# Filler matmuls in the waits of a router and sort, and a later turn back of the logits

## The chip, the cores and the metric

The kernel runs on one core of a Trainium2 chip. The metric is the time of one execution on the device, in microseconds (us). The core has five engines with a queue each: TensorE (PE, with its weight loads as PEld), VectorE (DVE), ScalarE (ACT), GpSimd (POOL) and the sync engine (SP), which here issues nearly all loads from HBM. An engine works through its queue in order, and waits where an instruction needs what another engine has not done yet.

## What is computed

Two layers of a decoder for 512 tokens of width 1024. The part of the reference that matters here is the mixture of experts that ends each layer: a router picks one of 4 groups and in it 2 of 8 experts for each token, the assignments are sorted by expert, and each expert works on its tokens.

```
for l in range(DEPTH):
    ...
    x = layer_norm(ALPHA * x + mixed @ w_out[l], ln_gain[l, 0], ln_bias[l, 0])
    ffn = hierarchical_moe(x, router_group_w[l], ...)
    x = layer_norm(ALPHA * x + ffn, ln_gain[l, 1], ln_bias[l, 1])

def hierarchical_moe(x, wg, bg, we, be, w_gate, w_up, w_down):
    g_logit = (xt @ wg) + bg
    _, g_idx = lax.top_k(g_logit, 1)
    e_logit = take_along_axis((xt @ we + be).reshape(n, 4, 8), g_idx)
    top_logit, top_local = lax.top_k(e_logit, 2)
    expert = g_idx * EXPERTS_PER_GROUP + top_local
    order = jnp.argsort(expert.reshape(n_assign), stable=True)
    counts = jnp.bincount(e_flat, length=N_EXPERTS)
    ...
    hdn = silu(xb @ w_gate[e]) * (xb @ w_up[e])
    return hdn @ w_down[e]
```

## The kernel before

**Tiles and stages.** The tokens lie in four tiles t = 0 to 3 of 128 rows. A layer has a dense part (projection, mixers, output projection, normalisation, router) and an expert part. The expert part first takes two fixed experts, whose weights are loaded ahead, and then 12 rounds of two or three experts each. Which experts those are is in `ids`, a small table that the sort of each layer makes; the sync engine reads it and only then issues the loads of a round's weights, each a tile of 1 MB, into 18 slots that come free as TensorE finishes with what lies in them.

**The loop over the tiles.** The second half of the output projection of a tile is a list of eight steps of three matmuls each (`gemm(t)`, `run(steps, n)` runs the next n). While TensorE runs the steps of tile t + 1, VectorE and ScalarE add and normalise tile t (`begin`, `over`; the last scaling is L934 and L935), TensorE turns the rows of tile t (`turned`, L1074, copied by L1082 and L1084), and `logits` multiplies them with the router's weights (L1093), one tile later. The logits come out with the experts along the partitions; VectorE copies them (L1098), and `back` turns them again (L1105, L1106), from where VectorE copies them into `L` (L1107). `choose` is a chain of ten small VectorE steps per tile that finds group and experts (L1134 to L1129).

**Router's end and sort.** After the last tile, `early` takes one PSUM bank `rp` from the four banks called g; columns 0 to 127 take the ranks of the four tiles (`rank`, L1170 and L1171), and further columns the counts and the sort's results (`count_up` L1177 and L1179, `sort_a` L1210 and L1211, `sort_b` L1223). VectorE reads that bank in `ranks` (L1185), `keys` (L1203, L1204), `sort_b` (L1218, L1221, L1222) and `sort_c`, whose first copy is `ids` (L1228). `onehots` (L1290) makes the one-hot rows that the first matmuls of the expert part need, the gather (L1330). The fixed experts' matmuls are L1370 and, after them, L1401.

**Order.** All of this is under a manual schedule: each engine's queue stands in the order in which the program is written, and the framework adds the waits that the use of tiles asks for. `warm(n)` puts n matmuls of the identity with itself into a fresh bank g whose result nobody reads; each is two MATMUL rows of the trace.

Of the kernel before, what the change touches and what calls it, by code (L numbers as in the profile page):

```python
# [162 lines left out]
class Trunk:  # L163
# [700 lines left out]
    def output(self, l):  # L864
# [47 lines left out]
        def gemm(t):  # L912

            ps = self.s()
            c = slice(128 * t, 128 * t + 128)

            def step(q, k):
                nc.tensor.matmul(ps, mh[:, k, c], wh[:, k, :], start=(q == 0), stop=False)
                nc.tensor.matmul(ps, mh[:, k, c], wl[:, k, :], start=False, stop=False)
                nc.tensor.matmul(ps, ml[:, k, c], wh[:, k, :], start=False, stop=(q == 7))  # L920

            return ps, [lambda q=q, k=k: step(q, k) for q, k in enumerate(korder)]

        def run(steps, n=99):
            while steps and n > 0:
                n -= 1
                steps.pop(0)()

        def over(t):
            st = sums[t]  # L930
            nm, sd, rs, nb = (st[:, n : n + 1] for n in (2, 4, 5, 6))
            V.reciprocal(rs, sd)
            V.tensor_mul(nb, nm, rs)
            V.tensor_scalar(self.xh(t, 0), self.xh(t, 0), nm, rs, OP.add, OP.mult)  # L934
            A.activation(self.xh(t, 1), self.xh(t, 1), AF.Identity, bias=nb, scale=rs)  # L935
# [27 lines left out]
        def begin(t, ps):  # L963
            add(t, 1, ps)
            apart(t, 1)

            st = sums[t]
            V.tensor_scalar(st[:, 7:8], st[:, 0:1], st[:, 1:2], 1.0 / (UP * D), OP.subtract, OP.mult)
            V.scalar_tensor_tensor(st[:, 5:6], st[:, 7:8], st[:, 7:8], st[:, 5:6], OP.mult, OP.add)
            self.centre(t, st)  # L970
            A.activation(st[:, 4:5], st[:, 4:5], AF.Sqrt, bias=st[:, 5:6], scale=UP**-2 / D)

        def rows(t, *engines):

            for h in range(2):
                high(t, h)
            for h in range(2):
                low(t, h, engines[h])
            for row, op in zip(tabs, (OP.mult, OP.add)):
                for h in range(2):  # L980
                    self.by_row(P, t, h, row, op)

        with self.manual(ET.PE):
            ps, steps = gemm(0)
            run(steps)
            for t in range(NT):
                last = t == NT - 1
                begin(t, ps)
                if not last:
                    ps, steps = gemm(t + 1)  # L990
                if t > 0:
                    lt = self.logits(t - 1, xt)
                if last:
                    self.back(2, lt)
                run(steps, 2)
                over(t)
                if 0 < t < 3:
                    self.back(t - 1, lt)
                if t == 2:
                    self.choose((0, 1))  # L1000
                if last:
                    self.choose((2,))
                    self.warm(6)
                run(steps, 4)
                xt = self.turned(t, A, A if last else V)
                rows(t, *((P, P) if last else (V, V)))
                run(steps)
            A.activation(sums[3][:, 3:4], self.eps, AF.Exp)
            self.warm(2)
            lt = self.logits(3, xt)  # L1010
            self.early()
            self.back(3, lt)
            self.warm(8)
            self.choose((3,), [lambda: self.ranks(0, 3)])
            self.oh16 = f[:, 5, :].bitcast(F16).rearrange("p (a t s) -> p a t s", a=2, t=NT)
            self.count_up()
            self.rank(NT - 1)
            self.keys()
            self.sort_a()
            self.places()  # L1020
            self.sort_b()
            self.warm(8)
            self.onehots(slice(0, 2))
            self.sort_c()
            self.onehots(slice(2, 4))
# [80 lines left out]
        nc.tensor.matmul(ps[:, 0:36], lt, self.two, start=False, stop=True)  # L1106
        nc.vector.tensor_copy(self.L[:, t, :], ps[:, 0:36])  # L1107

    def warm(self, n):

        if n:
            ps = self.g()
        for _ in range(n):
            self.nc.tensor.matmul(ps[:, 0:128], self.ident, self.ident, start=True, stop=True)

    def choose(self, tiles, more=()):

# [718 lines left out]
```

## Time and profile before

| | before |
|---|---|
| median of 3 runs | 1513.57 us (1512.85 to 1513.63) |
| profiled execution | 1514.36 us |
| its span, first to last instruction | 1512.7 us |
| TensorE busy | 1362.2 us (90%) |
| VectorE busy | 689.1 us (46%) |
| ScalarE busy | 395.2 us (26%) |
| GpSimd busy | 153.1 us (10%) |
| mean granted clock of TensorE | 0.956 |
| read from HBM | 441.45 MB, 293 GB/s over the span |

The times of the rows further down are counted from the start of the span. A granted clock of 1.00 is 2.4 GHz and 0.50 is 1.2 GHz, the two levels that TensorE's clock has. The profile divides the span into 40 slices of 37.8 us.

### The profile page before, as it was taken

What the parts mean: (1) busy time and instruction counts of PE and PEld (TensorE: products, weight loads), DVE (VectorE), ACT (ScalarE), POOL (GpSimd) and SP (SyncE); (2) the same over time, 40 slices, a digit from 0 to 9 for tenths busy, and PEclk for the clock granted to TensorE, in tenths of its full rate; (3) what the DMA queues carried; (4) which work ended last, traced back from release to release, by engine and by line L of the source; (5) the groups of instructions that cost most, each with busy time, mean ns of one, the idle gap of its engine ahead of it and who ended that gap; (6) DMA issues with size and microseconds to landing.
All of it is one profiled execution on the core that took longest, in us unless ns stands there. A gap on an engine that the chain in (4) does not pass through costs nothing. (4 is left out here: it accounts for less than half of the span.)

```text
span 1512.7 us, 22662 instructions
## 1 busy us (share of the span) xinstructions
PE 1362.2 (90%) x8836; PEld 755.1 (50%) x8837; DVE 689.1 (46%) x1540; ACT 395.2 (26%) x720; POOL 153.1 (10%) x188
## 2 busy tenths in 40 slices
PE   8999997899998988999699998979999989889994
PEld 7876576534343434343378665866343424343431
DVE  4347758524423242422553676585344242424225
ACT  5446544111010101011364555341110101010112
POOL 1112205100000000000141221050000000000001
PEclk9999999899999999999899998988999999999997
DMA  9410250799999999999911025408999999999994
GB/s 346 143 56 1 102 205 28 306 381 420 420 419 422 420 421 412 420 422 412 382 65 59 1 82 189 149 29 321 389 420 420 419 421 421 421 413 421 420 408 166
DMA packets 84550, 445.15 MB, mean 294 GB/s; under 512 B 8080, under 2 KB 14352, under 8 KB 36816
## 3 DMA queue, kind: packets, MB, share of 16 engines
q1 hardware_dynamic: 83184, 440.15, 72.5%
q0 software_dynamic: 960, 2.90, 0.6%
q8 instruction: 74, 1.21, 0.3%
q10 hardware_dynamic: 288, 0.52, 0.1%
q14 instruction: 44, 0.36, 0.1%
HBM read 441.45 MB, written 2.10 MB: 293 GB/s over the span
## 5 line engine op out<-in xcount | busy, mean ns | idle before, releaser
L1370 PE MATMUL g<-w,f 128*32 128x512 f32 (+1 forms) x3072 | 399.6, 595 | 13.7 <-DMA w<-expert_w_up 9.4
L1370 PEld LDWEIGHTS g<-w,f 128*32 128x32 f32 (+1 forms) x3072 | 120.8, 112 | 248.1 <-issue 202.4
L1401 PE MATMUL g<-w,f 128*32 128x512 f32 (+1 forms) x1536 | 211.6, 653 | 29.2 <-ACT f L1390 10.1
L1424 DVE TENSOR_TENSOR X<-X,s 128x512 f32<-128x512 f32 x176 | 113.0, 683 | 256.7 <-PE s L1419 256.7
L1401 PEld LDWEIGHTS g<-w,f 128*32 128x32 f32 (+1 forms) x1536 | 58.3, 121 | 161.7 <-issue 131.2
L1412 DVE SCALAR_TENSOR_TENSOR y<-g,gv,y 128x512 fp32r<-128x512 f32 x52 | 38.9, 750 | 212.1 <-ACT y L1411 209.8
L1419 PE MATMUL s<-y,fa 128*128 128x512 f32 x416 | 126.7, 425 | 6.4 <-DVE X L1424 3.5
L1419 PEld LDWEIGHTS s<-y,fa 128*128 128x128 f32 x416 | 70.1, 189 | 103.8 <-issue 71.9
L1411 ACT ACTIVATE y<-g,gv 128x512 fp32r<-128x512 f32 x52 | 35.5, 687 | 215.7 <-PE g L1401 215.7
L1330 PE MATMUL t<-fa,mh 128*128 128x256 f32 (+1 forms) x448 | 79.0, 298 | 8.9 <-ACT f L1390 8.8
L1341 ACT ACTIVATE f<-t,pp 128x256 f32<-128x256 f32 (+1 forms) x56 | 30.7, 549 | 206.7 <-PE t L1330 206.7
L1339 DVE TENSOR_SCALAR f<-t,pp 128x256 f32<-128x256 f32 (+1 forms) x56 | 29.4, 525 | 93.1 <-ACT f L1341 93.1
L1330 PEld LDWEIGHTS t<-fa,mh 128*128 128x128 f32 x448 | 61.3, 191 | 15.4 <-ACT f L1390 11.7
L1330 PE MATMUL t<-f,x1l 128*128 128x256 f16 (+1 forms) x448 | 64.9, 267 | 0.0
L1382 ACT ACTIVATE f<-g 128x512 f32<-128x512 f32 x26 | 15.6, 599 | 183.1 <-PE g L1370 183.1
L1530 POOL DMA_DIRECT2D rows<-ln_gain x2 | 1.1, 548 | 614.2 <-DMA w<-expert_w_gate 307.2
L1390 ACT COPY f<-t 128x512 f32<-128x512 f32 x26 | 15.2, 585 | 167.7 <-PE t L1389 167.7
L404 POOL TENSOR_TENSOR X<-X,f 128x512 f32<-128x512 f32 x32 | 40.5, 1296 | 87.9 <-DVE x1l L948 82.4
L404 POOL TENSOR_TENSOR X<-X,E 128x512 f32<-128x512 f32 x11 | 16.3, 1486 | 306.2 <-ACT X L1696 154.6
L701 ACT ACTIVATE f<-f,nm 128x128 f32<-128x128 f32 (+3 forms) x64 | 35.7, 558 | 43.7 <-POOL nm L700 42.9
L371 DVE TENSOR_TENSOR fa<-w,fa 128x512 fp32r<-128x512 f32 (+1 forms) x36 | 31.3, 877 | 32.0 <-ACT fa L370 31.9
L700 POOL TENSOR_SCALAR nm<-mx 128x1 f32<-128x1 f32 x64 | 22.3, 352 | 180.6 <-DVE mx L697 119.0
(338 smaller groups left out, 2165.5 us busy)
## 6 DMA issues: line engine op xcount, KB each, us to landing
w<-expert_w_gate SPq DMA_DIRECT2D x128, 1024.0 KB, 19.8
w<-expert_w_up SPq DMA_DIRECT2D x128, 1024.0 KB, 19.8
w<-expert_w_down SPq DMA_DIRECT2D x116, 1024.0 KB, 19.8
w<-w_in SPq DMA_DIRECT2D x20, 1024.0 KB, 13.6
w<-expert_w_down SPq DMA_DIRECT2D x48, 256.0 KB, 5.3
w<-w_out SPq DMA_DIRECT2D x8, 1024.0 KB, 5.3
X<-x SPq DMA_DIRECT2D x4, 512.0 KB, 5.9
w<-w_in SPq DMA_DIRECT2D x4, 512.0 KB, 8.2
```

The costliest lines, as they stand in the source:

```text
L371: self.nc.vector.tensor_sub(lo, src, hi.bitcast(F32))
L404: e.tensor_tensor(out=x, in0=x, in1=row[:, 512 * h : 512 * h + 512], op=op)
L701: nc.scalar.activation(p, p, AF.Exp, bias=nm, scale=0.125, accum_out=den)
L1330: nc.tensor.matmul(ps[:, w * j : w * j + w], src[:, k, 128 * t : 128 * t + 128], one[:, 0:n, t, :], start=(i == 0), stop=(i == 2 * NT - 1),)
L1339: nc.vector.tensor_scalar(xg[:, k, 0:w], src, gain(k), bias(k), OP.mult, OP.add)
L1341: nc.scalar.activation(xg[:, k, 0:w], src, AF.Identity, bias=bias(k), scale=gain(k))
L1370: nc.tensor.matmul(pss[m][a:b, :], xs[:, k, a:b], w[m][e][:, k, :], start=(k == 0), stop=(k == 7),)
L1401: nc.tensor.matmul(pss[hf][a:b, :], hT[:, 128 * j + a : 128 * j + b], part(e, hf, j), start=(j == 0), stop=(j == 3),)
L1411: nc.scalar.mul(yh, ps, gv)
L1412: nc.vector.scalar_tensor_tensor(yl, ps, gv, yh.bitcast(F32), OP.mult, OP.subtract)
L1419: nc.tensor.matmul(ps, oT[:, 128 * t : 128 * t + 128], y[q], start=(q == 0), stop=(q == 1))
L1424: nc.vector.tensor_add(x, x, ps)
```

## The change

In the loop four steps of the next tile's output products, instead of two, stand between the logits and their turn back, and two instead of four between that and the turn of the rows. `warm` can be given a place to write. Ahead of the turn back of tile 2 stand eight new filler matmuls, in a fresh bank g. After the turn back of tile 3 stand 24 instead of 8, ahead of `sort_a` 3, ahead of `sort_b` 8, and behind `sort_b` 14 instead of 8; all of these write columns 384 to 511 of the bank `rp`. Lines below L991 move by one to four, so that L1185 becomes L1189, L1218 becomes L1222 and L1228 becomes L1232.

```diff
                 if t > 0:
                     lt = self.logits(t - 1, xt)
                 if last:
+                    self.warm(8)
                     self.back(2, lt)
-                run(steps, 2)
+                run(steps, 4)
                 over(t)
                 if 0 < t < 3:
                     self.back(t - 1, lt)
...
                 if last:
                     self.choose((2,))
                     self.warm(6)
-                run(steps, 4)
+                run(steps, 2)
                 xt = self.turned(t, A, A if last else V)
...
             self.back(3, lt)
-            self.warm(8)
+            spare = self.rp[:, 384:512]
+            self.warm(24, spare)
             self.choose((3,), [lambda: self.ranks(0, 3)])
...
             self.keys()
+            self.warm(3, spare)
             self.sort_a()
             self.places()
+            self.warm(8, spare)
             self.sort_b()
-            self.warm(8)
+            self.warm(14, spare)
             self.onehots(slice(0, 2))
             self.sort_c()
             self.onehots(slice(2, 4))
...
-    def warm(self, n):
-
-        if n:
-            ps = self.g()
+    def warm(self, n, ps=None):
+
+        if ps is None and n:
+            ps = self.g()[:, 0:128]
         for _ in range(n):
-            self.nc.tensor.matmul(ps[:, 0:128], self.ident, self.ident, start=True, stop=True)
+            self.nc.tensor.matmul(ps, self.ident, self.ident, start=True, stop=True)
```

Three places show what this does to the queues. A row is an instruction with its line, its output and inputs; in brackets stand the engines (PE_49 is TensorE, DVE_49 VectorE) on which it waits.

VectorE at the choice of tile 3, first before, then changed: the copies of the logits, the first step of the choice, the read of the ranks of tiles 0 to 2 (`rk<-g,f`), and the next steps.

```order
L1107 COPY f<-t 128x36 [waits PE_49]
L1134 TENSOR_REDUCE rs<-f 128x1 [waits DVE_49]
L1185 SCALAR_TENSOR_TENSOR rk<-g,f 128x96
L1135 SCALAR_TENSOR_TENSOR f<-f,rs,tab 128x4 [waits DVE_49]
L1138 TENSOR_REDUCE rs<-f 128x1 [waits DVE_49]
L1139 TENSOR_SCALAR f<-f,rs 128x4 [waits DVE_49]
```

```order
L1111 COPY f<-t 128x36 [waits PE_49]
L1138 TENSOR_REDUCE rs<-f 128x1 [waits DVE_49]
L1189 SCALAR_TENSOR_TENSOR rk<-g,f 128x96 [waits PE_49]
L1139 SCALAR_TENSOR_TENSOR f<-f,rs,tab 128x4 [waits DVE_49]
L1142 TENSOR_REDUCE rs<-f 128x1 [waits DVE_49]
L1143 TENSOR_SCALAR f<-f,rs 128x4 [waits DVE_49]
```

The order is the same; the read of the ranks has gained a wait for TensorE.

TensorE in the sort, first before, then changed: the two matmuls of `sort_a`, that of `sort_b`, the fillers (`g<-ident`) and the first matmul of the gather.

```order
L1210 LDWEIGHTS onesb
L1210 MATMUL g<-f,onesb 128x32 [waits DVE_49]
L1211 LDWEIGHTS f
L1211 MATMUL g<-onesb,f 32x1
L1223 MATMUL g<-f,ones 128x96 [waits DVE_49]
L1114 MATMUL g<-ident 128x128 x8
L1330 MATMUL t<-fa,mh 128x128 [waits DVE_49,PE_49]
```

```order
L1118 MATMUL g<-ident 128x128 [waits DVE_49]
L1118 MATMUL g<-ident 128x128 x2
L1214 LDWEIGHTS onesb
L1214 MATMUL g<-f,onesb 128x32 [waits DVE_49]
L1215 LDWEIGHTS f
L1215 MATMUL g<-onesb,f 32x1
L1118 MATMUL g<-ident 128x128 [waits DVE_49]
L1118 MATMUL g<-ident 128x128 x7
L1227 MATMUL g<-f,ones 128x96 [waits DVE_49]
L1118 MATMUL g<-ident 128x128 x14
L1334 MATMUL t<-fa,mh 128x128 [waits DVE_49,PE_49]
```

The fillers of the sort wait for VectorE, and stand ahead of the sort's own matmuls.

VectorE in the sort, first before, then changed: the last step of `places`, the copies and comparisons of `sort_b`, the first one-hot, and `ids` with its neighbours.

```order
L1196 TENSOR_TENSOR u<-u,f 128x4 [waits DVE_49]
L1218 COPY f<-g 32x1
L1220 TENSOR_SCALAR f<-tab,f 32x32 [waits DVE_49]
L1221 TENSOR_SCALAR f<-g,tab 32x32
L1222 TENSOR_SCALAR f<-g,tab 32x32
L1290 TENSOR_TENSOR fa<-tab,u 128x256
L1228 CAST ids<-g 128x32 [waits PE_49]
```

```order
L1200 TENSOR_TENSOR u<-u,f 128x4 [waits DVE_49]
L1222 COPY f<-g 32x1 [waits PE_49]
L1224 TENSOR_SCALAR f<-tab,f 32x32 [waits DVE_49]
L1225 TENSOR_SCALAR f<-g,tab 32x32
L1226 TENSOR_SCALAR f<-g,tab 32x32
L1294 TENSOR_TENSOR fa<-tab,u 128x256
L1232 CAST ids<-g 128x32 [waits PE_49]
```

The copy at the start of `sort_b` has gained a wait for TensorE; `ids` had one before and has one now.

## Rows read from the trace of the kernel before

**Rows 1.** The page, 40 equal slices of the span: GB/s that the loads moved.

```profile
GB/s 346 143 56 1 102 205 28 306 381 420 420 419 422 420 421 412 420 422 412 382 65 59 1 82 189 149 29 321 389 420 420 419 421 421 421 413 421 420 408 166
```

**Rows 2.** Waits of the sync engine's queue, 268 to 345 us: total, times, longest.

```profile
SPq L357 <- PE g L1370: 26.9, 7, 8.4
SPq L309 <- DVE ids L1228: 23.4, 1, 23.4
SPq L357 <- PE g L1401: 22.6, 4, 12.1
```

**Rows 3.** Order in time, expert part's start: start us, us, engine, line, operation [idle before, releaser].

```profile
271.24 12.54 SPq L357 DMA_DIRECT2D w<-expert_w_gate  x6
...
279.76 7.09 PE L1370 MATMUL g<-w,f 128*64 128x512 f32 x32
```

**Rows 4.** Order in time, tile 1 of the loop.

```profile
231.95 0.41 PE L1106 MATMUL t<-f 128*128 128x36 f32 x2 [1.25 <-DVE f L1098]
...
232.73 1.60 DVE L934 TENSOR_SCALAR X<-X,su 128x512 f32<-128x512 f32 x1
...
235.03 1.04 PE L1074 MATMUL t<-ident,X 128*128 128x128 f32 x8
```

**Rows 5.** Order in time, tile 3 of the loop.

```profile
252.01 0.64 PE L1106 MATMUL t<-f 128*128 128x36 f32 x2 [2.28 <-DVE f L1098]
...
255.74 1.80 PE L1074 MATMUL t<-ident,X 128*128 128x128 f32 x8 [0.37 <-DVE rs L1134]
```

**Rows 6.** Order in time, the choice of tile 3.

```profile
259.93 2.03 PE L1114 MATMUL g<-ident 128*128 128x128 f32 x16
...
260.44 0.25 DVE L1185 SCALAR_TENSOR_TENSOR rk<-g,f 128x96 f32<-128x96 f32 x1
...
262.33 4.95 POOL L404 TENSOR_TENSOR X<-X,f 128x512 f32<-128x512 f32 x4
...
266.16 0.18 PE L1177 MATMUL g<-f,onesb 128*128 128x32 bf16 x1 [4.18 <-DVE f L1129]
```

**Rows 7.** Order in time, the sort and the gather's start.

```profile
267.37 0.18 PE L1210 MATMUL g<-f,onesb 32*128 32x32 bf16 x1 [0.72 <-DVE f L1205]
...
267.70 0.19 DVE L1185 SCALAR_TENSOR_TENSOR rk<-g,f 128x32 f32<-128x32 f32 x1 [0.38 <-PE g L1211]
...
268.55 0.14 DVE L1218 COPY f<-g 32x1 f32<-32x1 f32 x1
...
269.50 0.74 PE L1223 MATMUL g<-f,ones 32*128 32x96 f32 x2 [1.84 <-DVE f L1222]
...
270.17 3.78 PE L1114 MATMUL g<-ident 128*128 128x128 f32 x16
270.28 0.19 DVE L1228 CAST ids<-g 128x32 int32<-128x32 f32 x1 [0.50 <-PE g L1223]
...
270.58 0.41 DVE L1290 TENSOR_TENSOR fa<-tab,u 128x256 fp32r<-128x256 f32 x1
...
273.60 0.99 PE L1330 MATMUL t<-fa,mh 128*128 128x128 f32 x4
...
274.64 0.64 PE L1330 MATMUL t<-fa,mh 128*128 128x128 f32 x4
```

**Rows 8.** Short windows: busy us (instructions) of PE, PEld, DVE, ACT, POOL; PEclk, DMA share, GB/s.

```profile
250.00:252.00 2.00, 0.00 (x0) 0.00 (x0) 1.89 (x8) 0.91 (x3) 1.64 (x2) 0.61 0.45 188
...
264.00:266.00 2.00, 0.00 (x0) 0.00 (x0) 1.93 (x3) 0.00 (x0) 2.00 (x2) 0.52 0.00 0
...
274.00:276.00 2.00, 2.00 (x24) 2.00 (x24) 0.00 (x0) 0.38 (x1) 0.00 (x0) 0.92 0.98 397
```

**Rows 9.** Order in time, the choice of tile 2 and GpSimd's rows before it.

```profile
250.36 4.95 POOL L404 TENSOR_TENSOR X<-X,f 128x512 f32<-128x512 f32 x4 [5.39 <-PE t L1105]
...
255.69 0.22 DVE L1135 SCALAR_TENSOR_TENSOR f<-f,rs,tab 128x4 f32<-128x4 f32 x1
...
257.67 0.24 DVE L1129 TENSOR_SCALAR f<-f 128x32 bf16<-128x32 f32 x1
```

## The prediction

> **What bounds the kernel now.** I read the page's slices first, then the sync engine's waits at the start of the expert stage, then the order in time of one router, then the granted clock in short windows. The slices show a kernel of two equal halves. In each, TensorE works through the dense part while the loads rest, and then the expert weights stream at about 420 GB/s without a gap until that layer ends [rows 1]. So inside most of a layer's expert stage nothing but the loads counts, and the stage ends as much later as that gapless stream begins later. The stream is not gapless at once: its first two slices moved 306 and 381 GB/s [rows 1]. In that time the load queue waited first for `ids`, the table of experts that the sort makes, and then 26.9 + 22.6 us for TensorE to give weight slots back [rows 2]. What sets the time of a layer is thus TensorE's arrival at the expert matmuls (the first L1370, at 279.76), with `ids`, which released the first load at 271.24, as a second condition [rows 3]. Between the last output product and that point stands a chain of small work: VectorE's choice, two small matmuls, `keys`, two more, places, one more, `ids`, the gather. All of the change lies on or beside this chain, once in each layer; the second layer repeats the first there.
>
> **The change part by part**, for one layer, in microseconds, from the rows of the first.
>
> *Four steps instead of two.* In tile 1, TensorE stood 1.25 us before the turn back of the logits, because VectorE had not copied them; the steps that then ran kept it busy until 235.03, where it turned the next rows, though VectorE's scaling of them (232.73 + 1.60) was done at 234.33 [rows 4]. With two more steps in that wait the turn starts 235.03 − 234.33 = 0.7 earlier, and everything of the next tile follows. Tile 2 cannot add as much: VectorE has the choice of tiles 0 and 1 ahead of its next copy. **−0.7**, bounds 0 and −1.4.
>
> *Eight fillers ahead of the turn back of tile 2.* They stand in a wait of 2.28 us [rows 5]. A filler is two rows of the trace; 16 rows took 2.03 us at the full clock, so 0.254 each [rows 6], and 3.78 at half, 0.472 each [rows 7]. Eight take 2.03 and fit; at half they would stick out by 1.5. What they may give is the clock, which fell to half around 250.4 (a mean of 0.61 from 250 to 252) [rows 8]: the turn back took 0.64 there against 0.41 at full, the eight transposes 1.80 against 1.04 [rows 4, 5]. All of it would be 0.23 + 0.76 = −1.0; the pause before it in tile 2 gets longer, so I take half, **−0.5**.
>
> *Twenty-four fillers ahead of the choice of tile 3.* Here the place of the output decides. They write columns 384 to 511 of the PSUM bank that also holds the ranks. In the order of the changed program VectorE's read of the ranks (L1189, formerly L1185), which waited for nothing, now waits for TensorE, and in the built program the count it waits for is the one that the 24th filler raises. The rest of the choice is queued behind it on VectorE, and the whole sort waits for the choice. The fillers end at 259.93 + 24 × 0.254 = 266.02; the read stood at 260.44, so VectorE stops for 5.6. Part comes back: the choice of one tile took from 260.44 to 266.10 because VectorE's steps met GpSimd's four row operations of 262.33 to 267.28 [rows 6], while tile 2's same steps needed 255.69 to 257.91 = 2.2, after GpSimd's last four had ended at 255.31 [rows 9]. After: 266.05 + 0.16 + 2.2 = 268.4, and up to one operation of GpSimd (1.24) later, so +2.3 to +3.6 against 266.10; I take **+2.6**, near the lower end, since GpSimd is nearly done by then.
>
> *Three fillers before the first sort matmul.* TensorE waited 0.72 there, to the end of `keys` [rows 7]. The three take 0.76 but cannot start before the second step of `keys`, whose read of the same bank they wait for; about half of them lies beside the third step. **+0.35**, at half clock +1.0.
>
> *Eight before the next.* They wait for the rank read at 267.70 + 0.19, and `sort_b`'s copy out of the same bank (L1222, formerly L1218, at 268.55) now waits for them: 267.94 + 2.03 = 269.97. **+1.4**, at half clock +3.2 [rows 7]. The matmul behind it (L1223, 0.74 at half) gains at most half of that at full clock; I take **−0.25**.
>
> *Fourteen instead of eight before the gather.* The old eight used a bank of their own and ran at half clock: the gather began right behind them, 270.17 to 273.60 = 3.43 [rows 7]. Fourteen take 3.56 at full, 0.13 more. But they too lie in the rank bank, so the cast of `ids`, at 270.28 before, comes behind all fourteen, and the second one-hot, which the gather's third matmul needs, stands behind that cast on VectorE: 270.28 to 270.99, 0.7 more. **+0.85**, at half clock +3.9. The gather's first four matmuls at full clock (0.99 against 0.64 [rows 7]): **−0.35**.
>
> Sum at full clock: −0.7 − 0.5 + 2.6 + 0.35 + 1.4 − 0.25 + 0.85 − 0.35 = **+3.4** at L1370.
>
> *The clock.* TensorE fell idle at 261.98 and was granted half from about 264.1, 2.1 us later; full came back at about 274.3, 4.8 us after it resumed with L1223 at 269.50 [rows 6 to 8]. In the changed kernel it is idle from 266.02 to about 268.7, 2.7 us, as VectorE only starts the choice then. So the fillers do not remove the pause, they move it, and I take the fall as likely. With half clock for 4.8 us from there the three cost 0.65 more; of the eight, which start some 2.85 in (0.8 to the three, 1.4 for them, 0.65 for two matmuls and the rank read), four run at half: 0.9 more. **+1.55**. The upper end, all 25 at half, is 0.65 + 1.75 + 3.05 = +5.45.
>
> *How it passes on.* L1370 is 3.4 + 1.55, say 5.0 later. `ids` is later by the parts up to L1223 (−1.2 + 2.6 + 0.35 + 1.4 = 3.15), by 3.2 for the fourteen ahead of its cast (0.4 + 3.56 against 0.78 before) and by 1.55 for the clock: 7.9. The difference, 2.9, is taken up by the load queue: it waits for TensorE soon after its first loads in any case [rows 2], and the two weak slices are short of 420 GB/s by (114 + 39) / 420 × 37.8 = 13.8 us (a slice is 37.8), of which 6.5 lie ahead of the first load and some 7 behind it [rows 1, 3]. So each layer ends 5.0 later. Two layers: **+10.0**. Against the profiled execution that is 1514.36 + 10.0 = 1524.4; the median of the runs is 0.8 lower, so 1523.6.
> The Trainium skill (PSUM — Partial Sum Buffer, PSUM bank collisions raise a hardware error) says to guard PSUM by bank and quadrant, not by address. By that rule a filler in a spare column of the rank bank holds up the reads of the ranks; the order of the program, where both reads gained a wait, agrees, and no run shows yet what it costs.
>
> **The rivals.**
> *Faster.* The waits cost nothing, and only the gains stay: the turn (−0.7), the clock in the last tile (−1.0), in the sort and the gather (−0.37, −0.35), 2.4 a layer: 1508.7. It needs the read of the ranks to be free by about 263.3 (266.10 less 2.2 less 0.16, less the gains ahead of it), so fillers twice as short as the rows show, or a wait on an earlier count. For it speaks that GpSimd already stretched the choice to 5.66; against it, that 24 × 0.254 is longer than even that. Chance 0.05.
> *It does not reach the end.* The later arrival is swallowed by the gaps of the early stream: 1513.6. For it speak the two weak slices; against it, that the queue's waits there end with TensorE, which is late itself [rows 2]. Chance 0.06.
> *`ids` passes on in full.* The first five loads fill slots that are free before TensorE needs any, so a late `ids` could push the whole stream: 7.9 a layer, 1529.4. Against it: the long waits for TensorE behind them. Chance 0.08.
> *Half clock throughout.* All fillers of the sort at half: 3.4 + 5.45 = 8.85 a layer, 1531.3; with the 24 at half too (24 × 0.218 = 5.2 more) 1541.7. For it speaks that the clock was at half before, down to the transposes of 255.74 [rows 5, 8]; against it, that a run of 24 keeps TensorE busy. Chance 0.11, two thirds of it within the range.
>
> **How the numbers follow.** The forecast, later by the waits on the bank with the clock fallen for part of the sort, has 0.70, with a fifth of it for a clock that stays full (+6.8, 1520.4). Its own bounds: all lower ends give −1.4 − 1.0 + 2.3 + 0.35 + 1.4 − 0.37 + 0.85 − 0.35 = 1.8 a layer, 1517.2, and the choice's upper end with a longer stretch of half clock about 8, 1529.6. With the rival on `ids` and the lower part of that on the clock the range 1517.5 to 1531.5 leaves out some 2 in 10. A measurement of this kernel can tell about 0.2% (3 us) from no change. Faster by more 0.05; within it 0.07 (the swallowed delay, and a sum near its lowest end); slower 0.88.
>
> **What would show it.** In the profile after: L1189 begins when the last of 24 fillers ends, some 4 to 6 us after the choice's first step; the choice behind it takes about 2.2 to 3 instead of 5.66; TensorE pauses 2 to 3 us behind the fillers, and the clock falls in or after it; L1222 and the cast of `ids` begin behind the last of 8 and of 14; the first load is 6 to 9 later and L1370 4 to 6. The turn of tile 1 begins as VectorE's scaling ends. I am wrong if L1189 starts beside the fillers, or if L1370 is late and the last output is not.

## The result, and the profile after

| | before | changed |
|---|---|---|
| median of 9 runs each | 1513.75 us | 1523.75 us (1520.45 to 1533.07) |
| changed over before | | 1.0064, 95% interval 1.0048 to 1.0081 |
| profiled execution, its span | 1514.36, 1512.7 us | 1525.47, 1523.8 us |
| TensorE busy, mean granted clock | 1362.2 us, 0.956 | 1376.9 us (90%), 0.968 |

The change makes the kernel slower by 10.0 us, although TensorE's mean clock is higher. One of the nine runs of the kernel before took 1584.94 us; the ratio is taken without it. The page's slices, which answer to [rows 1], still show two equal halves with the gapless stream at about 420 GB/s; the eighth slice, in which the first layer's stream begins, moved 247 GB/s instead of 306.

```profile
GB/s 346 139 55 1 96 209 28 247 390 419 420 421 420 421 421 413 421 419 417 380 74 58 1 84 194 139 28 297 388 419 421 420 420 420 421 414 420 420 408 157
```

The sync engine's waits from 268 to 345 us of the changed kernel (total, times, longest) answer to [rows 2]: the wait for `ids` is 9.3 longer, and those for TensorE are 4.7 shorter, but still there.

```profile
SPq L309 <- DVE ids L1232: 32.7, 1, 32.7
SPq L357 <- PE g L1374: 24.1, 7, 6.5
SPq L357 <- PE g L1405: 20.7, 3, 12.1
```

The loop, in order of time (start, us, engine, line and operation, idle before and releaser): tile 1, then tile 3, for [rows 4, 5]. This profiled run is 1.3 us later than that of before already at VectorE's addition of tile 1 (L901 at 231.35 against 230.05), so distances are compared from there.

```profile
233.26 0.41 PE L1110 MATMUL t<-f 128*128 128x36 f32 x2
...
235.78 1.06 PE L1078 MATMUL t<-ident,X 128*128 128x128 f32 x8 [0.66 <-DVE f L1111]
...
252.78 0.41 PE L1110 MATMUL t<-f 128*128 128x36 f32 x2 [0.51 <-DVE f L1102]
...
255.27 1.07 PE L1078 MATMUL t<-ident,X 128*128 128x128 f32 x8 [0.66 <-DVE rs L1138]
...
258.11 2.99 POOL L948 TENSOR_TENSOR x1l<-X,mh 128x512 f16<-128x512 f32 x2 [1.86 <-ACT mh L944]
258.30 1.37 DVE L1135 TENSOR_TENSOR f<-f 128x32 bf16<-128x32 bf16 x1
...
259.92 0.41 PE L1110 MATMUL t<-f 128*128 128x36 f32 x2 [1.16 <-DVE f L1102]
```

The turn of tile 1 comes 4.43 after that addition instead of 4.98 (behind VectorE's scaling it still waited for the copy L1111), and in tile 3 the turn back and the transposes take 0.41 and 1.07, the times of the full clock. The eight fillers ran at 250.07 for 2.05 and fit into the wait. New is the last step of tile 2's choice, L1135: it met two operations of GpSimd and took 1.37, and the turn back of tile 3 waited 1.16 for what stands behind it.

The choice of tile 3, the sort and the gather's start, for [rows 6, 7, 3]:

```profile
260.17 5.61 PE L1118 MATMUL g<-ident 128*128 128x128 f32 x48
...
261.18 4.93 POOL L404 TENSOR_TENSOR X<-X,f 128x512 f32<-128x512 f32 x4
...
265.81 0.26 DVE L1189 SCALAR_TENSOR_TENSOR rk<-g,f 128x96 f32<-128x96 f32 x1 [5.05 <-PE g L1118]
...
268.24 0.18 PE L1181 MATMUL g<-f,onesb 128*128 128x32 bf16 x1 [1.95 <-DVE f L1133]
...
269.03 1.65 PE L1118 MATMUL g<-ident 128*128 128x128 f32 x6 [0.34 <-DVE f L1208]
...
270.62 0.20 PE L1214 MATMUL g<-f,onesb 32*128 32x32 bf16 x1
...
271.21 3.78 PE L1118 MATMUL g<-ident 128*128 128x128 f32 x16 [0.28 <-DVE rk L1189]
...
275.03 0.15 DVE L1222 COPY f<-g 32x1 f32<-32x1 f32 x1 [3.14 <-PE g L1118]
...
276.00 0.46 PE L1227 MATMUL g<-f,ones 32*128 32x96 f32 x2 [1.00 <-DVE f L1226]
...
276.38 3.39 PE L1118 MATMUL g<-ident 128*128 128x128 f32 x28
...
279.81 0.19 DVE L1232 CAST ids<-g 128x32 int32<-128x32 f32 x1 [3.54 <-PE g L1118]
...
280.58 0.44 PE L1334 MATMUL t<-fa,mh 128*128 128x128 f32 x2 [0.64 <-DVE fa L1294]
...
280.78 9.51 SPq L357 DMA_DIRECT2D w<-expert_w_gate  x6
...
286.27 4.08 PE L1374 MATMUL g<-w,f 128*64 128x512 f32 x18
```

Three reads on VectorE (L1189, L1222 and `ids`) now begin where a group of fillers ends, after waits of 5.05, 3.14 and 3.54 us for nothing but L1118. The short windows, for [rows 8], show the granted clock (third number from the end): the half clock of before in the last tile is gone, and the one in the sort begins later, at about 268.7, and lasts 6.8 us. (A window of 2 us with a mean of 0.68 was at half for 4 × 0.32 = 1.28 of them.)

```profile
250.00:252.00 2.00, 2.00 (x20) 1.93 (x18) 1.93 (x6) 0.19 (x1) 0.88 (x1) 1.00 0.54 225
...
266.00:268.00 2.00, 0.18 (x1) 0.10 (x1) 1.72 (x10) 0.00 (x0) 0.11 (x1) 1.00 0.00 0
268.00:270.00 2.00, 1.42 (x9) 1.19 (x9) 0.66 (x4) 0.00 (x0) 0.00 (x0) 0.68 0.00 0
...
274.00:276.00 2.00, 1.00 (x6) 0.71 (x5) 0.93 (x5) 0.00 (x0) 0.00 (x0) 0.61 0.00 0
```

The next table cuts the way from VectorE's addition of tile 1 (L901) to the first expert matmul (L1374, or L1370 before) into steps, in us of the first layer, for the two kernels and three experiments below. A step ends where the next row's begins.

| step | before | changed | own_24 | bridge | own_bank |
|---|---|---|---|---|---|
| to the addition of tile 3 | 20.09 | 19.55 | 19.60 | 19.57 | 19.57 |
| to the copy of its logits (L1102) | 9.20 | 8.69 | 8.71 | 8.72 | 8.71 |
| to the end of the choice | 6.76 | 8.60 | 7.09 | 8.60 | 7.09 |
| to `sort_a` (L1214) | 1.27 | 2.43 | 1.71 | 1.71 | 1.21 |
| to `sort_b`'s copy (L1222) | 1.18 | 4.41 | 2.66 | 2.66 | 1.17 |
| to its matmul (L1227) | 0.95 | 0.97 | 0.96 | 0.96 | 1.03 |
| to the expert matmuls | 10.26 | 10.27 | 10.28 | 10.28 | 9.34 |
| sum, first layer | 49.71 | 54.92 | 51.01 | 52.50 | 48.12 |
| sum, second layer | 49.54 | 54.78 | 50.83 | 52.35 | 48.01 |

So a layer reaches its expert matmuls 5.2 us later. The spans' difference of 11.1 is 1.30 (ahead of tile 1) + 5.21 − 1.67 (first layer's expert part) − 0.12 (second layer's dense part) + 5.24 + 1.14 (second expert part). Those small terms also move between kernels whose router is alike (see the end).

### The profile page after: what moved, and what is told of

It reads as the page before. It is cut to its first block, busy times and chain, and to the rows that moved or that the text cites. A ratio compares the mean times of both kernels' runs of the same rounds, so it can differ in the third digit from the quotient of the medians.

```text
span 1523.8 us, 22988 instructions
## 1 busy us (share of the span) xinstructions
PE 1376.9 (90%) x9000; PEld 767.6 (50%) x9001; DVE 684.6 (45%) x1540; ACT 395.1 (26%) x720; POOL 152.9 (10%) x188
## 3 DMA queue, kind: packets, MB, share of 16 engines
q8 instruction: 74, 1.21, 0.3%
## 5 line engine op out<-in xcount | busy, mean ns | idle before, releaser
L1374 PE MATMUL g<-w,f 128*32 128x512 f32 (+1 forms) x3072 | 401.2, 595 | 15.9 <-DMA w<-expert_w_up 9.9
L1374 PEld LDWEIGHTS g<-w,f 128*32 128x32 f32 (+1 forms) x3072 | 119.5, 112 | 252.4 <-issue 205.5
L1405 PEld LDWEIGHTS g<-w,f 128*32 128x32 f32 (+1 forms) x1536 | 55.4, 116 | 160.2 <-issue 126.5
L404 POOL TENSOR_TENSOR X<-X,f 128x512 f32<-128x512 f32 x32 | 40.9, 1309 | 86.3 <-DVE x1l L948 80.7
L404 POOL TENSOR_TENSOR X<-X,E 128x512 f32<-128x512 f32 x11 | 15.8, 1443 | 305.4 <-ACT X L1700 155.6
L1118 PE MATMUL g<-ident 128*128 128x128 f32 x276 | 40.1, 306 | 1.2 <-DVE f L1208 0.7
## 6 DMA issues: line engine op xcount, KB each, us to landing
w<-w_in SPq DMA_DIRECT2D x20, 1024.0 KB, 13.6
```

Of the source, the lines that this page charges most:

```text
L404: e.tensor_tensor(out=x, in0=x, in1=row[:, 512 * h : 512 * h + 512], op=op)
L1118: self.nc.tensor.matmul(ps, self.ident, self.ident, start=True, stop=True)
L1374: nc.tensor.matmul(pss[m][a:b, :], xs[:, k, a:b], w[m][e][:, k, :], start=(k == 0), stop=(k == 7),)
L1405: nc.tensor.matmul(pss[hf][a:b, :], hT[:, 128 * j + a : 128 * j + b], part(e, hf, j), start=(j == 0), stop=(j == 3),)
```

## The experiments

The theory: VectorE's reads of the rank bank wait for the fillers that write beside what they read, and the stop that this makes lets TensorE's clock fall. Rivals: the number of fillers or the clock costs the time, wherever they write; and `ids`, not TensorE's arrival, sets the layer's end. Diffs are against the changed kernel unless another is named. Times are medians; the ratios are to the kernel before on the same chip. "To the experts" is the sum of the table above.

**own_bank.** All four groups of the sort write a spare bank.

```diff
-            spare = self.rp[:, 384:512]
+            spare = self.g()[:, 0:128]
```

> The changed kernel, with the 24, 3, 8 and 14 fillers writing one spare bank of their own instead of columns 384 to 511 of the rank bank; the fillers and all else stay. My theory (VectorE's reads of the rank bank wait for the fillers): L1189, L1222 and ids no longer wait for them, the choice, the sort and the gather lose 2.2 + 3 + 0.6 us a layer at the least, TensorE has no pause of over 1 us behind the 24 and keeps the full clock, and what is left of the change are its gains of 0.5 to 2 us a layer: 1510 to 1513 us, at most the kernel before. Rival (the number of fillers or the clock costs, wherever they write): the time stays within 2 us of the changed kernel, 1521 to 1524.

1509.01 us, ratio 0.9965 (0.9952 to 0.9978): below the kernel before. The same 49 fillers, and no wait for them; to the experts 48.1 and 48.0. The rows (order in time):

```profile
259.64 4.94 POOL L404 TENSOR_TENSOR X<-X,f 128x512 f32<-128x512 f32 x4
259.81 1.12 DVE L1143 TENSOR_SCALAR f<-f,rs 128x4 f32<-128x4 f32 x1
260.96 1.21 DVE L1144 TENSOR_TENSOR f<-f 128x32 f32<-128x32 f32 x1
...
268.92 3.39 PE L1118 MATMUL g<-ident 128*128 128x128 f32 x28
269.03 0.19 DVE L1232 CAST ids<-g 128x32 int32<-128x32 f32 x1 [0.29 <-PE g L1227]
...
272.07 0.64 PE L1334 MATMUL t<-fa,mh 128*128 128x128 f32 x4
```

`ids` waits for the sort's own matmul alone, and the granted clock is 1.00 in every window from 244 to 290 us. The place of the output is what costs; the rival is out. Two things stay to be had: the choice's steps beside GpSimd's row operations (L1143, L1144) take 1.1 to 1.2, and the gather waits for nothing but the fourteen fillers.

**own_24.** Only the 24 in a spare bank (`self.warm(24, own)`), the others in the rank bank.

> The changed kernel, with only the 24 fillers ahead of the choice of tile 3 in a spare bank of their own; the 3, 8 and 14 still write the rank bank. My theory, in its two parts: the stop of the choice costs 2.2 us a layer, and the pause that it makes on TensorE lets the clock fall, which costs another 0.9 on the 3 and 1.75 on the 8 fillers. So 2.2 + 2.6 = 4.8 a layer less than the changed kernel, 1514; the clock stays full from 268 to 276. Rival (the clock falls anyway, or its fall is not due to that pause): only 2.2 a layer, 1519. If the stop costs nothing at the end: 1523.

1518.89 us, ratio 1.0027 (1.0014 to 1.0040), with a spread of 1514.1 to 1524.5. To the experts 51.0 and 50.8, so the 24's place costs 54.9 − 51.0 = 3.9 a layer, where 4.8 was expected: 1.5 in the choice, not 2.2, then 0.7 ahead of `sort_a` and 1.75 ahead of `sort_b`. In the table these last two are the half clock, which this kernel's profile shows nowhere from 244 to 290 us. What is left of the bank, at full clock, is 0.5 for the 3, 1.5 for the 8 and 0.94 for the 14 (against own_bank). The median, though, is what the rival had forecast (1519), and some 2 us above what the profile's 1.3 a layer, twice, gives, for the profiled run is the shortest of twelve. So the time alone does not decide here; **own_24_again** took a second trace, and bridge, below, puts the question another way.

> own_24 once more, for its trace. Its 12 runs spread from 1514.1 to 1524.5 us, with a mean granted clock of 0.976 in the shortest and 0.962 in the longest. If the spread is the clock in the router and the sort: a run of over 1518 us has half clock somewhere from 255 to 290 or from 1010 to 1050 us, which the run of 1514.1 had nowhere, and its way from the second tile's addition to the expert matmuls is 2 to 6 us longer than 51.0 in that layer. If it is elsewhere: that way is 51 us in both layers, and the difference lies in the expert stage or the dense part.

A run of 1517.44 us: 51.0 and 51.4 to the experts, which is nearer the second case. Of the 3.3 us that it is longer, 2.2 stand behind the second layer's expert matmuls (479.4 to the end against 477.2). So most of what this run is longer by is not in the router; the six runs above 1518.2 have no trace, and half clock in the router of some of them is not excluded. Its second layer shows half clock inside the 24 fillers, from about 1014.2 to 1017.6, and they took 7.23 instead of 5.61.

**bridge.** The stop parted from the clock.

```diff
             self.warm(24, spare)
+            self.warm(10, own)
```

> The changed kernel with ten more fillers, in a spare bank of their own, right behind the 24: VectorE still stops until the 24th ends, but TensorE is busy while the choice then runs (ten take 2.3 us, the pause was 2.3). It parts the stop from the clock. In the profiles the 24 in the rank bank cost 3.9 us a layer against own_24, of which 1.4 stand at the end of the choice, and 2.5 behind it, on the 3 and the 8 fillers at half clock. My theory (the pause lets the clock fall): the clock stays full, the 3 take 0.7 and the 8 take 1.75 less, 52.4 us from the second tile's addition to the expert matmuls instead of 54.9, about 1519. Rival (the clock falls for another reason, or ten more matmuls only hold up the sort): 54.9 or more, 1524 or more.

1519.59 us, ratio 1.0031 (1.0020 to 1.0043); to the experts 52.5 and 52.4. Order in time (lines one lower in this file), then the windows:

```profile
257.80 7.84 PE L1119 MATMUL g<-ident 128*128 128x128 f32 x68
...
263.44 0.26 DVE L1190 SCALAR_TENSOR_TENSOR rk<-g,f 128x96 f32<-128x96 f32 x1 [5.05 <-PE g L1119]
...
265.88 0.18 PE L1182 MATMUL g<-f,onesb 128*128 128x32 bf16 x1 [0.23 <-DVE f L1134]
```

```profile
268.00:272.00 4.00, 2.89 (x22) 2.61 (x23) 1.82 (x10) 0.40 (x1) 0.00 (x0) 1.00 0.00 2
```

VectorE's wait of 5.05 is the same, TensorE's pause shrinks from 1.95 to 0.23, and the clock does not fall: 2.4 us a layer come back with ten matmuls more. That the pause lets the clock fall in the changed kernel is shown, in both layers of the two traces, and its price with it.

**twice_24.** 48 instead of 24, in the rank bank (`self.warm(48, spare)`).

> The changed kernel with 48 instead of 24 fillers in the rank bank ahead of the choice of tile 3. A filler took 0.234 us there, so VectorE's read of the ranks begins 5.6 us later. My theory (the stop is on the path, and from 24 on GpSimd has nothing more to give back, as its row operations ended with the 24th): all 5.6 pass on, 60.5 us from the second tile's addition to the expert matmuls, 1535. Rival (part of it is taken up by the loads or by GpSimd): under 58 us or under 1530.

1535.51 us, ratio 1.0128 (1.0108 to 1.0149); to the experts 59.3 and 59.2.

```profile
260.33 10.96 PE L1118 MATMUL g<-ident 128*128 128x128 f32 x96
...
271.33 0.26 DVE L1189 SCALAR_TENSOR_TENSOR rk<-g,f 128x96 f32<-128x96 f32 x1 [10.41 <-PE g L1118]
```

The wait doubles, and the choice ends 5.4 later, as the 24 more take. One us of it came back in the sort: the clock fell later and was at half for 3.4 instead of 6.8 us, so the 3 fillers ran at full. Nothing else takes a longer stop up.

**own_14.** Only the 14 in a spare bank (`self.warm(14, own)`); `ids` no longer behind them.

> The changed kernel, with only the 14 fillers behind the sort in a spare bank of their own, so that the copy to ids is 3 us earlier, while TensorE still runs the 14 ahead of the gather. My theory (TensorE's arrival at L1374 sets the layer's end): only the gather's wait for the second one-hot goes, 0.6 a layer, 1522 to 1523. Rival (ids passes on in full): 3 a layer, 1517 to 1518.

1524.65 us, ratio 1.0063 (1.0040 to 1.0087): not faster than the changed kernel, though `ids` stood 3 us earlier, and the rival on `ids` is out. In the first layer 54.1 to the experts, 0.8 less (0.6 was expected); in the second 57.1, and why shows in the order in time and the window of that layer:

```profile
1035.93 6.30 PE L1118 MATMUL g<-ident 128*128 128x128 f32 x28
1036.03 0.19 DVE L1232 CAST ids<-g 128x32 int32<-128x32 f32 x1 [0.50 <-PE g L1227]
...
1041.92 0.70 PE L1334 MATMUL t<-fa,mh 128*128 128x128 f32 x4
```

```profile
1038.00:1042.00 4.00, 4.00 (x22) 4.00 (x20) 0.00 (x0) 0.00 (x0) 0.00 (x0) 0.50 0.90 358
```

There the clock stayed at half to 1042, and all fourteen ran at it, 6.3 us in which nothing else stood in TensorE's way. Of the six runs three took 1520.0 to 1522.2 and three, the profiled one among them, 1527.1 to 1531.8; even the former do not reach the rival's 1517 to 1518.

**loop_only.** The kernel before with the change in the loop alone.

```diff
                 if last:
+                    self.warm(8)
                     self.back(2, lt)
-                run(steps, 2)
+                run(steps, 4)
...
-                run(steps, 4)
+                run(steps, 2)
```

> The kernel before, with the loop's part of the change alone: four and two steps instead of two and four, and eight fillers in a fresh bank ahead of the turn back of tile 2. My theory: the turn of tile 1 is 0.55 earlier and the last tile runs at the full clock, 0.5 to 1.5 us a layer less, 1510.5 to 1512.5. Rival (the 1.37 us step of the choice beside GpSimd, or VectorE's queue, takes it back): 1513 to 1514.

1514.87 us, ratio 1.0000 (0.9992 to 1.0009). The time does not change; the forecast was missed, and the rival came nearer. The gain is there, 1.0 us at the copy of tile 3's logits, but only 0.4 to 0.5 of it reaches the experts (49.2 and 49.2). GpSimd's row operations come earlier too and meet more of the choice, which takes 7.07 instead of 6.76; and the half clock of the sort ends when it did before (0.92 from 274 to 276 in both), so the gather, now earlier, has more of it and takes 0.36 longer.

**no_fill.** The changed loop without any filler behind the turn back of tile 3, those of before included.

```diff
-            self.warm(24, spare)
...
-            self.warm(3, spare)
...
-            self.warm(8, spare)
...
-            self.warm(14, spare)
```

> The changed loop with no fillers at all behind the turn back of tile 3: no 24, 3, 8 and 14, nor the 8 and 8 of the kernel before. My theory (fillers are worth the clock): TensorE falls idle for 6 us in the choice and is at half clock through the sort and for some 5 us of the gather; the gather starts about 40.3 us behind the second tile's addition and takes 8 to 10 instead of 5.8: 48.5 to 50.5 us to the expert matmuls, 1511 to 1515, behind own_bank. Rival (the clock is worth nothing there): 46.2 us, 1505 to 1506.

1519.14 us, ratio 1.0037 (1.0022 to 1.0053), worse than expected. The gather starts at 39.3, earlier than expected, and takes 11.1:

```profile
268.00:272.00 4.00, 3.81 (x22) 3.62 (x23) 0.91 (x5) 0.86 (x2) 0.00 (x0) 0.50 0.50 158
272.00:276.00 4.00, 4.00 (x27) 4.00 (x26) 0.55 (x2) 0.46 (x1) 0.00 (x0) 0.50 1.00 414
```

The clock stays at half through the whole gather and beyond it, to about 282.6. So fillers are worth having here: 50.4 to the experts, and the first layer's expert part, begun at half clock, takes 465.2 us where the other kernels take 461.4 to 463.9; that part I had not counted.

**own_4.** own_bank with 4 instead of 14 behind the sort.

```diff
-            self.warm(14, spare)
+            self.warm(4, spare)
```

> own_bank with 4 instead of 14 fillers behind the sort. There the gather's first matmul stood 3.53 us behind the sort's last one, for the fillers alone: the second one-hot was ready 1.2 us behind it. My theory (with the clock kept up, fillers beyond the wait only hold TensorE): the gather starts 2.1 us earlier and the clock stays full, 46.0 instead of 48.1 us from the second tile's addition to the expert matmuls, 1505. Rival (the 14 are needed to keep the clock): half clock in the gather, 48 to 50 us, 1509 to 1513.

1506.80 us, ratio 0.9946 (0.9934 to 0.9959); 45.9 and 45.8 to the experts, the clock at 1.00 through both routers. Fourteen were too many by about ten.

**rows_last.** own_4's tail, GpSimd's row operations of tile 3 behind the one-hots, and 10 fillers ahead of the choice (against own_bank).

```diff
+            if t < NT - 1:
+                scaled(t)
+        def scaled(t):
             for row, op in zip(tabs, (OP.mult, OP.add)):
                 for h in range(2):
                     self.by_row(P, t, h, row, op)
...
-            self.warm(24, spare)
+            self.warm(10, spare)
...
-            self.warm(14, spare)
+            self.warm(4, spare)
...
             self.onehots(slice(2, 4))
+            P.tensor_copy(self.rt[:, 601:602], self.fa[:, 0, 511:512].bitcast(F32))
+            scaled(3)
```

> own_bank with GpSimd's four row operations of tile 3 (L404) issued behind the last one-hot instead of ahead of the choice (one tiny copy on GpSimd waits for the one-hot), with 10, 3, 8 and 4 fillers, as the choice is then short. In own_bank four of the choice's steps took 0.96 to 1.21 us while L404 ran, and 0.2 to 0.3 elsewhere; in the changed kernel, where the stop let GpSimd finish first, the same choice took 2.4 us. My theory (GpSimd stretches the choice by 4.1 us): the choice takes 2.4 to 3 us, the sort stands 4 us earlier, 41.5 to 42.5 us to the expert matmuls, 1495 to 1499. Rival (those steps are slow for another reason, or the gather's copies meet L404 in their place): 45 to 46 us, 1503 to 1505, as own_4.

1502.19 us, ratio 0.9915 (0.9902 to 0.9928), the fastest; 42.3 and 42.2 to the experts. The same steps as in own_bank's rows (six lines lower in this file), and where GpSimd's operations went:

```profile
258.88 0.23 DVE L1149 TENSOR_SCALAR f<-f,rs 128x4 f32<-128x4 f32 x1
259.15 0.19 DVE L1150 TENSOR_TENSOR f<-f 128x32 f32<-128x32 f32 x1
...
265.56 4.96 POOL L404 TENSOR_TENSOR X<-X,f 128x512 f32<-128x512 f32 x4
```

1.12 and 1.21 became 0.23 and 0.19, and the choice takes 2.45 from the read of the ranks on, against 2.38 behind the stop of the changed kernel and 6.0 in own_bank. The fewer fillers are not the reason: in no_fill, which has none there, the choice took 7.07, as in loop_only. The gather's copies beside L404 kept their 0.41. It is own_4 less 3.6 a layer at the experts; 4.6 us of those 7.2 reach the median, which misses the 1495 to 1499 expected: the profile's second expert part took 482.2 us where own_4's took 479.0, and why was not tested.

## Why the prediction was right

**What bounds the kernel.** Right. The row of the load queue with the gate tiles that begins at 489.08 before begins at 495.62 in the changed kernel; behind its first expert matmul that is 209.32 and 209.35 us. In own_14, own_24, own_bank and loop_only it is 209.26 to 209.38, while `ids` stood 6.5 to 9.9 us ahead of those matmuls. (In no_fill, whose first expert matmuls still ran at half clock, it is 211.68: TensorE's pace just behind its arrival counts too.) So the stream hangs on TensorE's arrival one to one, and a late `ids` was taken up as forecast.

**The terms**, forecast and measured in the table, per layer:

| term | forecast | measured |
|---|---|---|
| four steps instead of two | −0.7 | −0.54 |
| eight fillers, last tile | −0.5 | −0.51 |
| 24 fillers and the choice | +2.6 | +1.84 |
| three, with its part of the clock | +0.35 + 0.65 | +1.16 |
| eight, with its part of the clock | +1.4 + 0.9 | +3.23 |
| L1227, fourteen, the gather | −0.25 + 0.85 − 0.35 | +0.03 |
| sum | +4.95 | +5.21 |
| `ids` | +7.9 | +8.2 |

*The 24.* The mechanism is as described: the read begins as the 24th filler ends, and the choice behind it takes 2.38 (forecast 2.36) instead of what GpSimd made of it. This is the term that was mis-sized: 1.84 lies below its lower bound of 2.3, since a filler in a long row took 5.61 / 24 = 0.234, not the 0.254 of a group of eight [rows 6], 0.5 less in all.

*The clock.* It fell behind the 24, as taken for likely: at 268.7, half a us after a pause of TensorE that lasted from 265.8 to 268.2 but for one matmul of 0.18. The forecast had full clock back 4.8 us after work resumed; it took 7.3, of which 6.8 at half, so all of the eight ran at half and not four. bridge prices the fall at 54.92 − 52.50 = 2.4 where the sum had 1.55. The two errors, −0.76 and +0.87 a layer, all but cancel: that the sum is so close is luck, though the range had them both.

*The eight in the loop.* They kept the clock in the last tile, whole. That their term came out at the half that I had set is luck. Besides the clock's 1.0 another 0.93 came from a step of VectorE that met GpSimd's row operations before and no longer did (first before, then changed):

```profile
252.99 1.09 DVE L933 TENSOR_TENSOR su<-su 128x1 f32<-128x1 f32 x1
```

```profile
253.53 0.16 DVE L933 TENSOR_TENSOR su<-su 128x1 f32<-128x1 f32 x1
```

The new meeting of L1135 with GpSimd took 1.4 back: the copy of tile 3's logits (L1102) began 1.44 behind the last matmul of these logits, where it had been 0.03. So what the forecast put down to the longer pause is two meetings with GpSimd, one gone and one new.

*The skill's rule.* The Trainium skill (PSUM — Partial Sum Buffer, PSUM bank collisions raise a hardware error) has PSUM guarded by bank and quadrant. The traces agree: VectorE's reads waited 5.05, 3.14 and 3.54 us for writes to other columns of their bank, and for fillers in a bank of their own not at all. What these runs show is the waits that the program was built with, not what the bank itself would do.

*GpSimd.* That the choice was stretched by GpSimd's row operations, a step of the forecast, was read from two rows; rows_last showed it. (Not all of it was the four operations named there: L1139, which took 1.24 from 261.04, was over before they began at 262.33; it lay beside L948, GpSimd's operation ahead of them.) The Trainium skill (SBUF — State Buffer, SBUF: two separate sides) says that VectorE and GpSimd share a port pair, which a GpSimd operation, or a VectorE operation in a two-port mode or with two inputs in SBUF, holds for its whole length while the other is blocked. The trace of own_bank agrees: beside four operations of 1.24 four steps of the choice took 0.96 to 1.21, and a search for the maximum among them (MAX8, L1149) 0.20 as ever.

*The rivals.* "Faster" names what own_bank is: without the waits the change is 5 us faster, not slower. `ids` passing on in full is refuted by own_14, a swallowed delay by twice_24. Half clock throughout did not come in the changed kernel's profile; own_14's second layer shows that such a layer can, at 57.1.

## What to carry to other kernels

Give filler matmuls a PSUM bank that nobody reads, and look in the built order whether a read has gained a wait for them: here the same change was worth −5 or +10 us by the fillers' bank alone. Size each group to the pause that it fills, from rows of a dense group, and no longer: every one beyond it stood in the way of the next real matmul, while a pause of some 2 us left unfilled cost another 2.4. Before filling a wait, ask what makes it long; moving four operations of another engine out of a chain of small VectorE steps brought 3.6 us a layer up to the expert matmuls.

## What was not expected of the hardware

- How long the half clock lasts, counted from its fall, differs between routers of alike work: 6.8 us in all in the changed kernel's first layer and in own_14's, 13.6 in own_14's second, 23.9 in no_fill, where TensorE was busy without a gap for the last 14 of them. No experiment explains it; it stays open.
- The clock fell inside a dense group of fillers too (own_24_again, at 1014.2, 0.3 us into the group and 0.5 behind a wait of 1.16), and came back within it 3.4 us later.
- The expert parts, the same program in nearly all of these kernels, differ by up to 3 us (461.4 to 463.9 in the first layer, 477.1 to 479.9 in the second, leaving out no_fill's first and rows_last's second). The longer ones have short dips of the clock near the layer's end (0.91 over 20 us, from 680 and from 720 us, in the kernel before; none there in the changed one). In the first layer that parts all twelve traces: the four with 461.4 (changed, own_bank, own_24 and own_24_again) show no half clock from 605 to 735 us, the eight with 462.6 and more do. This is the likely source of much of the runs' spread of 2 to 13 us, and of own_bank's 2 us beyond its gain at the experts; whether the dips make these parts longer was not tested.
